# Gated DeltaNet layer: decay masks by GpSimd selection, and the inverse's 64-row block transposed by VectorE

## The chip, the cores and the metric

The kernel runs on one core of a Trainium2 chip. The metric is the device time of one execution in microseconds, the median of three runs. Five engines work side by side: TensorE (PE in the profile, its weight loads PEld), VectorE (DVE), ScalarE (ACT), GpSimd (POOL) and SyncE (SP), which here does nothing but issue DMAs. Each takes its instructions in the order in which they were written and waits on semaphores for the others.

## The reference

One decoder layer over 2048 tokens of width 1024, in float32. The token mixer is a gated DeltaNet of 8 heads of 128, beside it a cross-attention of 4 heads to 256 memory tokens; both read one projection of x, and their outputs are concatenated and projected. Then come a layer norm, an MLP with a squared ReLU (4096 wide) and a second layer norm. The part that matters here is the chunked delta rule, cut to its core:

```
gc = jnp.cumsum(to_chunks(g), axis=-1)
decay = jnp.exp(jnp.where(causal, gc[..., :, None] - gc[..., None, :], -jnp.inf))
lower = jnp.where(strict, jnp.einsum('bnhcd,bnhsd->bnhcs', k_beta, kc) * decay, 0.0)
a_mat = jnp.eye(CHUNK, dtype=f32) + lower
u = lax.linalg.triangular_solve(a_mat, v_beta, ...)
w = lax.linalg.triangular_solve(a_mat, k_beta * jnp.exp(gc)[..., None], ...)
attn_qk = jnp.einsum('bnhcd,bnhsd->bnhcs', qc, kc) * decay
```

and then, chunk by chunk, a state of 128 x 128 per head is read and updated. So each head needs two tables of decays (one strictly lower, one with the diagonal) and, for each chunk, the inverse of a unit lower triangular matrix.

## The kernel before

**Tiling.** Tokens are worked in four blocks of 512 (loop over b at L1111). The kernel uses chunks of 128 tokens in place of the reference's 64, which is the same recurrence, so a block has four chunks per head, side by side in one tile of 128 x 512 (v4, L392). The large matmuls split each float32 operand into a high and a low part of type float32r and add three products (mm3, L468); the high part is a ScalarE cast, the low part a VectorE difference (split, L450), for weights as for activations. The tile of split weights is called whl in the profile, the raw one wraw.

**A block.** For each head, dense (L673) projects q, k, v and z, runs the short convolution (raw, with three tokens of halo copied in by GpSimd) and makes the head's row scales (rk, vbs, bh, nbe) on GpSimd from sums of squares (ss) at L718 to L729. gdn_a (L818) makes the decay tables dl and at, multiplies them with the products of k and q (pkq) and calls invert. gdn_b (L869) runs the four chunks through the state. In step t of the loop at L1127, gdn_b of head t-2, gdn_a of head t-1 and dense of head t are written down one after another; four memory attentions go into the last steps. Then come the output projection (L1141), the layer norm and the MLP (ff_seven, L991).

**The decay tables.** Tile gb holds, in every partition, the cumulated gate of the block's tokens, spread by a DMA (L824). VectorE adds a mask tile m_l (1e30 on and above the diagonal) or m_at (-1e30 below it), repeated for the four chunks, and ScalarE takes the exponential chunk by chunk, with the partition's own gate as the bias.

**invert (L732).** The 128 x 128 triangular matrices of four chunks are inverted together. First all 16-row diagonal blocks, by a substitution of 15 steps on VectorE (shuffle, multiply, subtract on tiles Bc and Xc). Then three rounds of block merging: 16 to 32, 32 to 64, 64 to 128 rows. Each round is two groups of four small float32 matmuls: pq from the off-diagonal block, copied to Q by ScalarE, and pp from the diagonal inverse and Q. The matmul takes its first operand transposed, so each round needs the transposed inverse so far (XB, X32, X64), while Y3 gathers the result. In the last round the 64-row blocks of Y3 are transposed by TensorE into px and copied into X64 by VectorE. pq, px and pp of a head all live in the one PSUM bank of its parity ("ga0" or "ga1"), one after another.

**FF2.** ff_seven multiplies 2 x 2 blocks with seven products instead of eight, accumulating three PSUM results A, B and C (A in the "ga" banks, B and C in the two "pb" banks), which are added to the output tile after every product that contributes. SEVEN (L987) lists the seven in order: left operand, right operand, result, whether it goes on from the last content of the bank, and the output block. Right operands 1 to 4 are sums of weight blocks. In block 0 VectorE makes them (keep_sums, L971) and a DMA writes them to the DRAM scratch tsc, from which they're read there and in the later blocks; B11, B21 and B22 are read as they are.

**What sets the order.** Nothing is issued where it is written. A Recorder (L135) collects all instructions with their data dependences, prices each with a formula of its own (cost, L184), and plays the program as a list schedule (issue, L220): of the instructions that are ready on an engine, the one written first goes next, and tile buffers are handed out in order of first use. The resulting order is then emitted, all of it at L320, which is why most rows of the profile have this line; they're told apart by tile names. The prices decide only the order; on the chip the semaphores decide the times.

## Time and profile before

| | |
|---|---|
| median of three runs | 2998.03 us (2996.6 to 2998.27) |
| the profiled execution | 2999.08 us, its span 2997.4 us |
| granted TensorE clock, mean | 0.995 |
| TensorE busy | 2945.4 us (98%) |
| VectorE busy | 2168.6 us (72%) |
| ScalarE busy | 1520.3 us (51%) |
| GpSimd busy | 332.4 us (11%) |

A row of the profile gives line, engine, operation, output tile and input tiles, shapes, the count, then busy time in us and the mean ns of one, then the idle time of the engine ahead of these instructions and what ended most of it. Matmuls are pipelined: one lasts longer than the distance to the next, so the busy time of a group is less than count times mean. Rows of waits give who waited for whom, the total in us, how often, and the longest. Rows of a timeline give start and duration in us.

### The profile page before, as it was taken

To read this page: it belongs to the slowest core of one execution; us is meant where nothing else is said; L and a number is where in the kernel's file an instruction comes from. 1 tells how busy PE (TensorE), PEld (TensorE's weight loads), DVE (VectorE), ACT (ScalarE), POOL (GpSimd) and SP (SyncE) were. 2 spreads that over 40 slices of the span, in tenths; PEclk is the share of its full clock that TensorE was granted. 3 is DMA by queue.
4 is the path that set the end of the run, shared out by engine and by line. 5 is a ranking of instruction groups with operands and counts; after the bars stand their busy time and mean duration, and the time that the engine had idled before them with its cause. 6 is when DMAs were issued, how large, how long until landed. Compare 5 with 4: busy or idle time off the path is not lost.

```text
span 2997.4 us, 43880 instructions
## 1 busy us (share of the span) xinstructions
PE 2945.4 (98%) x15300; PEld 2428.1 (81%) x15300; DVE 2168.6 (72%) x5537; ACT 1520.3 (51%) x3582; POOL 332.4 (11%) x808
## 2 busy tenths in 40 slices
PE   7999999999999999999999999999999999999998
PEld 6888788888788878888878887888878888788886
DVE  6898977666777787655577887665667787675667
ACT  5676534544355562544445665344554556444443
POOL 1222100000112211000012221000001222000000
PEclk9999999999999999999999999999999999999999
DMA  6765566656733223444473332244446332324443
GB/s 231 253 218 180 196 209 224 200 183 192 268 142 132 106 89 102 145 137 133 151 268 130 121 119 92 87 152 144 145 159 250 126 134 96 99 88 146 143 147 134
DMA packets 127709, 469.85 MB, mean 157 GB/s; under 512 B 14464, under 2 KB 16896, under 8 KB 109056
## 3 DMA queue, kind: packets, MB, share of 16 engines
q1 hardware_dynamic: 126912, 467.00, 46.2%
q8 instruction: 120, 1.97, 0.3%
q14 instruction: 101, 0.83, 0.1%
q10 hardware_dynamic: 576, 0.06, 0.0%
HBM read 402.97 MB, written 64.03 MB: 156 GB/s over the span
## 4 chain that ended last, share of the span: by engine, by line
PE 88%; DVE 8%; ACT 2%; issue 1%; DMA 1%; POOL 0%; POOLq 0%; ACTq 0%; DVEq 0%; SPq 0%
PE af L320 42%; PE ao L320 8%; PE aq L320 6%; PE ak L320 5%; PE az L320 5%; PE av L320 4%; PE amq L320 3%; PE pc L320 3%; PE pp L320 2%; PE pq L320 2%; PE po L320 2%; PE pkq L320 1%; DVE y L320 1%; PE sps L320 1%; DVE ck L320 1%
## 5 line engine op out<-in xcount | busy, mean ns | idle before, releaser
L320 DVE TENSOR_TENSOR whl<-wraw,whl 128x1024 fp32r<-128x1024 f32 (+1 forms) x446 | 538.7, 1216 | 392.8 <-ACT whl L320 386.1
L320 PE MATMUL af<-Thi,whl 128*128 128x512 f32 (+1 forms) x2304 | 655.9, 369 | 6.9 <-DVE whl L320 4.0
L320 ACT CAST whl<-wraw 128x1024 fp32r<-128x1024 f32 (+1 forms) x446 | 466.1, 1045 | 381.8 <-PE af L320 169.0
L320 PEld LDWEIGHTS af<-Thi,whl 128*128 128x128 f32 x2304 | 421.7, 191 | 78.5 <-DVE whl L320 4.8
L320 PE MATMUL af<-whl,xh 128*128 128x512 f32 x1536 | 476.4, 391 | 3.6 <-DVE whl L320 3.6
L320 PE MATMUL af<-Tlo,whl 128*128 128x512 f32 (+1 forms) x1152 | 424.8, 369 | 0.0
L320 PE MATMUL af<-whl,xl 128*128 128x512 f32 x896 | 347.3, 390 | 0.0
L320 PEld LDWEIGHTS af<-whl,xh 128*128 128x128 f32 x1536 | 288.6, 188 | 68.6 <-DVE whl L320 6.7
L320 PE MATMUL ao<-whl,ch 128*128 128x512 f32 x768 | 249.4, 399 | 0.5 <-DVE y L320 0.5
L320 PEld LDWEIGHTS af<-Tlo,whl 128*128 128x128 f32 x1152 | 220.4, 191 | 34.8
L320 ACT ACTIVATE rl<-af 128x512 f32<-128x512 f32 x128 | 76.5, 598 | 271.0 <-PE af L320 269.0
L320 DVE SCALAR_TENSOR_TENSOR y<-y,af 128x512 f32<-128x512 f32 x224 | 151.3, 684 | 84.1 <-PE af L320 82.9
L320 PEld LDWEIGHTS af<-whl,xl 128*128 128x128 f32 x896 | 168.5, 188 | 35.5
L320 POOL TENSOR_SCALAR ve<-mv 128x1 f32<-128x1 f32 x34 | 23.3, 684 | 1528.8 <-DVE mv L320 1528.8
L320 PE MATMUL aq<-Thi,whl 128*128 128x512 f32 x512 | 181.6, 414 | 7.5 <-ACT Thi L320 7.5
L320 PE MATMUL av<-Thi,whl 128*128 128x512 f32 x512 | 173.0, 402 | 0.0
L320 PE MATMUL ak<-Thi,whl 128*128 128x512 f32 x512 | 172.9, 401 | 0.0
L320 PE MATMUL az<-Thi,whl 128*128 128x512 f32 x512 | 170.2, 400 | 0.0
L320 PEld LDWEIGHTS ao<-whl,ch 128*128 128x128 f32 x768 | 142.6, 188 | 27.0 <-DVE y L320 0.7
L320 PE MATMUL ao<-whl,cl 128*128 128x512 f32 x384 | 153.5, 400 | 0.0
L320 PEld LDWEIGHTS aq<-Thi,whl 128*128 128x128 f32 x512 | 94.3, 192 | 21.5 <-ACT Thi L320 7.5
L320 PEld LDWEIGHTS az<-Thi,whl 128*128 128x128 f32 x512 | 95.9, 190 | 18.8 <-DVE whl L320 0.5
(252 smaller groups left out, 5756.3 us busy)
## 6 DMA issues: line engine op xcount, KB each, us to landing
wraw<-in_w_ff_dram SPq DMA_DIRECT2D x224, 512.0 KB, 4.0
whl<-wsc SPq DMA_DIRECT2D x108, 1024.0 KB, 4.8
wraw<-tsc SPq DMA_DIRECT2D x128, 512.0 KB, 3.3
wsc<-whl SPq DMA_DIRECT2D x36, 1024.0 KB, 4.9
wraw<-in_w_out_dram SPq DMA_DIRECT2D x48, 512.0 KB, 4.1
wraw<-in_w_in_dram SPq DMA_DIRECT2D x35, 512.0 KB, 5.8
wq<-in_w_ff_dram SPq DMA_DIRECT2D x64, 256.0 KB, 4.3
tsc<-wq SPq DMA_DIRECT2D x64, 256.0 KB, 3.3
```

Of the source, the lines that this page charges most:

```text
L320: o.fn(*[res(a) for a in o.args], **{k: res(v) for k, v in o.kw.items()})
```

## The change

The tiles m_at and m_l are gone, and so is the addition on VectorE. GpSimd's affine_select copies gb into dl (or at) and fills the masked places with 1e30 (or -1e30) as it goes, by comparing partition and column, over all four chunks in one instruction. The planner gets a price for it.

In invert, X64 is no longer the transposed 64-row block of Y3. Its two diagonal blocks of 32 rows are copied from Z by GpSimd, right behind the same copies into X32. Its off-diagonal block is the transposed pp of the round before: VectorE transposes it in 32 x 32 squares out of PSUM (into t32, which lies in the buffer of Lq, unused by then), and a second VectorE instruction writes it, times -1, into X64. The four TensorE transposes into px and the copy of px are gone.

In FF2, for the first group of the first block alone, the seven products are taken in another order: A12 x B21, the sixth, comes second.

Besides, a padding tile of 112 columns and its memset are gone, and the two buffers of raw become 56 columns longer each, so that the tiles behind them lie at other addresses.

```diff
@@ -215,6 +215,8 @@
             return 300 + 165 * n
         if name == "tensor_copy":
             return 119 + 3.34 * n
+        if name == "affine_select":
+            return 90 + 1.6 * n
         return 150 + 2.1 * n if name == "tensor_tensor" else 176 + 3.34 * n
 
     def issue(self):
@@ -369,8 +371,6 @@
     cst = ctx.enter_context(tc.tile_pool(name="cst", bufs=1))
     wp = ctx.enter_context(tc.tile_pool(name="wp", bufs=1))
     tp = ctx.enter_context(tc.tile_pool(name="tp", bufs=1))
-    pad = ctx.enter_context(tc.tile_pool(name="pad", bufs=1))
-    nc.vector.memset(pad.tile([P, 112], F32, name="shift"), 0.0)
     sp = ctx.enter_context(tc.tile_pool(name="sp", bufs=1))
     sm = ctx.enter_context(tc.tile_pool(name="sm", bufs=1))
     ps = ctx.enter_context(tc.tile_pool(name="ps", bufs=1, space=bass.MemoryType.PSUM))
@@ -400,14 +400,6 @@
     triu = cst.tile([P, P], F32, name="triu")
     nc.gpsimd.affine_select(out=triu, in_=ones, compare_op=ALU.is_ge, fill=0.0,
                             base=0, pattern=[[1, P]], channel_multiplier=-1)
-    m_at = cst.tile([P, P], F32, name="m_at")
-    nc.gpsimd.memset(m_at, 0.0)
-    m_l = cst.tile([P, P], F32, name="m_l")
-    nc.gpsimd.memset(m_l, 0.0)
-    nc.gpsimd.affine_select(out=m_at, in_=m_at, compare_op=ALU.is_ge, fill=-1e30,
-                            base=0, pattern=[[1, P]], channel_multiplier=-1)
-    nc.gpsimd.affine_select(out=m_l, in_=m_l, compare_op=ALU.is_gt, fill=1e30,
-                            base=0, pattern=[[-1, P]], channel_multiplier=1)
     half = cst.tile([P, 2], F32, name="half")
     nc.vector.reduce_sum(out=half, in_=ident.rearrange("p (q h i) -> p h q i", h=2, i=16),
                          axis=AX.XY)
@@ -683,8 +675,8 @@
                 nc.vector.scalar_tensor_tensor(out=c, in0=th, scalar=1.0, in1=a, op0=ALU.add, op1=ALU.mult)
             else:
                 gi = o // P + h
-                raw = rec.buf(tp, (P, TB + 3), F32, "raw", 2, "raw")
-                nc.scalar.copy(out=raw[:, 3:], in_=a)
+                raw = rec.buf(tp, (P, TB + 3 + 56), F32, "raw", 2, "raw")
+                nc.scalar.copy(out=raw[:, 3:TB + 3], in_=a)
                 nc.gpsimd.tensor_copy(raw[:, 0:3], halo[:, gi].part(gi))
                 if b < NB - 1:
                     nc.gpsimd.tensor_copy(halo[:, gi].part(gi), raw[:, TB:TB + 3])
@@ -780,26 +772,27 @@
         nc.vector.transpose(Z.rearrange("p c f -> p (c f)"), ZT.rearrange("p c f -> p (c f)"))
         for p in range(2):
             nc.vector.tensor_copy(X32[32 * p:32 * p + 32, :, 32 * p:32 * p + 32], Z[64 * p:64 * p + 32])
+            nc.gpsimd.tensor_copy(X64[32 * p:32 * p + 32, :, 32 * p:32 * p + 32], Z[32 * p:32 * p + 32])
         for r in quads:
             nc.scalar.copy(out=Y3[r, :, r], in_=ZT[r])
         pq = bank("pq", "ga%d" % par)[:64, :P].rearrange("p (c f) -> p c f", c=NC)
         for c in range(NC):
             nc.tensor.matmul(pq[:, c], L32[:, c], ZT[:, c], start=True, stop=True)
         nc.scalar.copy(out=Q[:64, :, :32], in_=pq)
-        pp = bank("pp", "ga%d" % par)[:64, :P].rearrange("p (c f) -> p c f", c=NC)
+        p32 = bank("pp", "ga%d" % par)
+        pp = p32[:64, :P].rearrange("p (c f) -> p c f", c=NC)
         for c in range(NC):
             nc.tensor.matmul(pp[:, c], X32[:, c], Q[:, c, :32], start=True, stop=True)
+        t32 = Lq[:32].rearrange("p f c -> p (f c)")
+        nc.vector.transpose(t32, p32[:32, :P])
         for p in range(2):
             nc.vector.tensor_scalar_mul(Y3[64 * p:64 * p + 32, :, 64 * p + 32:64 * p + 64],
                                         pp[32 * p:32 * p + 32], -1.0)
+        nc.vector.tensor_scalar_mul(X64[32:64, :, :32], t32.rearrange("p (c f) -> p c f", c=NC), -1.0)
 
         pq = bank("pq", "ga%d" % par)[:64, :2 * P].rearrange("p (c f) -> p c f", c=NC)
         for c in range(NC):
             nc.tensor.matmul(pq[:, c], L[:, c, :64], Y3[:, c, 64:], start=True, stop=True)
-        px = bank("px", "ga%d" % par)[:64, :2 * P].rearrange("p (c f) -> p c f", c=NC)
-        for c in range(NC):
-            nc.tensor.transpose(px[:, c], Y3[:64, c, :64], ident[:64, :64])
-        nc.vector.tensor_copy(X64[:64], px)
         nc.scalar.copy(out=Q[:64], in_=pq)
         pp = bank("pp", "ga%d" % par)[:64, :2 * P].rearrange("p (c f) -> p c f", c=NC)
         for c in range(NC):
@@ -834,12 +827,14 @@
         bh, vbs = r["bh"], r["vbs"]
         dl = slot("dl", "s%d" % par)
         dl3 = v4(dl)
-        nc.vector.tensor_tensor(out=dl3, in0=gb3, in1=m_l.unsqueeze(1).to_broadcast([P, NC, P]), op=ALU.add)
+        nc.gpsimd.affine_select(out=dl3, in_=gb3, compare_op=ALU.is_gt, fill=1e30,
+                                base=0, pattern=[[0, NC], [-1, P]], channel_multiplier=1)
         for c in range(NC):
             nc.scalar.activation(dl3[:, c], dl3[:, c], AF.Exp, bias=sc("gc", c), scale=-1.0)
         at = slot("at", "s%d" % par)
         at3 = v4(at)
-        nc.vector.tensor_tensor(out=at3, in0=gb3, in1=m_at.unsqueeze(1).to_broadcast([P, NC, P]), op=ALU.add)
+        nc.gpsimd.affine_select(out=at3, in_=gb3, compare_op=ALU.is_ge, fill=-1e30,
+                                base=0, pattern=[[0, NC], [1, P]], channel_multiplier=-1)
         for c in range(NC):
             nc.scalar.activation(at3[:, c], at3[:, c], AF.Exp, bias=sc("ngc", c))
         kh, kl = r["kq"]
@@ -973,7 +968,7 @@
         if j == 0:
             B = [t[:, n * TB:(n + 1) * TB].part(n) for t in (tok_tile("wq"), tok_tile("wq")) for n in range(2)]
         else:
-            B = [rec.buf(tp, (P, TB + 3), F32, "raw", 2, "wq")[:, :TB] for _ in range(2)]
+            B = [rec.buf(tp, (P, TB + 3 + 56), F32, "raw", 2, "wq")[:, :TB] for _ in range(2)]
             kq = rec.buf(tp, (P, 2, TB), F32, "kq1", 1, "wq")
             B += [kq[:, n].part(n) for n in range(2)]
         for n in range(4):
@@ -1039,7 +1034,8 @@
             if last:
                 gb = load_bcast(ln2_g, "l2g"), load_bcast(ln2_b, "l2b")
             banks = {}
-            for n, (xn, wn, bn, on, (th, nh)) in enumerate(SEVEN):
+            order = [0, 5, 1, 2, 3, 4, 6] if b == 0 and g == 0 else range(7)
+            for n, (xn, wn, bn, on, (th, nh)) in enumerate(SEVEN[i] for i in order):
                 if not on:
                     banks[bn] = [bank("af2", ("ga%d" % t) if bn == "A" else "pb") for t in range(2)]
                 w = [None, None]
```

## The prediction

> **What bounds the kernel now.** I read the page first, then the list of who waited for whom on TensorE, then the windows.
>
> ```profile
> span 2997.4 us, 43880 instructions
> ...
> PE 2945.4 (98%) x15300; PEld 2428.1 (81%) x15300; DVE 2168.6 (72%) x5537; ACT 1520.3 (51%) x3582; POOL 332.4 (11%) x808
> ...
> PEclk9999999999999999999999999999999999999999
> ...
> PE 88%; DVE 8%; ACT 2%; issue 1%; DMA 1%; POOL 0%; POOLq 0%; ACTq 0%; DVEq 0%; SPq 0%
> ```
>
> TensorE is busy for 2945.4 of 2997.4 us, at nearly full clock throughout; the chain that ended last runs 88% through it. 52 us are left in which it does nothing. So a shorter VectorE, ScalarE or GpSimd instruction is worth only what it takes out of those 52 us, and a TensorE instruction that is dropped is worth its own slot. The waits say how little the first kind can be:
>
> ```profile
> PE af L320 <- DVE whl L320: 7.6, 10, 1.5
> PE aq L320 <- ACT Thi L320: 7.5, 1, 7.5
> ...
> PE pp L320 <- ACT Q L320: 1.6, 6, 0.3
> ...
> PE pkq L320 <- ACT jq L320: 1.2, 1, 1.2
> PE pc L320 <- ACT vt L320: 1.2, 5, 0.4
> ...
> PE pq L320 <- DVE Bc L320: 1.1, 3, 0.4
> ```
>
> (total us, times, longest.) In the chunk stage, the place of the change, the quoted waits of pp, pkq, pc and pq come to 1.6 + 1.2 + 1.2 + 1.1 = 5.1 us in all 32 head-blocks together. The long one, 7.5 us, is the start, where ScalarE's first cast is awaited. In the windows a GDN stretch of the second block looks like this (us; busy us of PE, PEld, DVE, ACT, POOL; clock; DMA share; GB/s):
>
> ```profile
> 800.00:1090.00 290.00, 286.44 (x1679) 234.82 (x1678) 224.99 (x863) 168.25 (x562) 63.48 (x175) 1.00 0.37 133
> ```
>
> TensorE 99% busy, VectorE 225/290 = 78%, GpSimd 22%: the dense projections fill TensorE's time while the heads' chains run.
>
> **Part 1: the 64-row block's transposes leave TensorE.** Per head-block four px transposes, their copy out of PSUM and the bank's hand-over go.
>
> ```profile
> L320 PE MATMUL px<-ident,Y 64*64 64x64 f32 x128 | 14.3, 224 | 0.0
> ```
> ```profile
> 2581.85 0.40 PE L320 MATMUL ao<-whl,cl 128*128 128x512 f32 x1
> 2582.18 0.41 PE L320 MATMUL px<-ident,Y 64*64 64x64 f32 x4
> 2582.52 0.74 PE L320 MATMUL ao<-whl,ch 128*128 128x512 f32 x2
> 2583.10 0.40 PE L320 MATMUL ao<-whl,cl 128*128 128x512 f32 x1
> 2583.34 0.40 PE L320 MATMUL ao<-whl,ch 128*128 128x512 f32 x1
> 2583.66 0.50 PE L320 MATMUL pp<-Q,X 128*64 128x64 f32 x5
> ```
> ```profile
> 508.96 0.39 PE L320 MATMUL af<-whl,xl 128*128 128x512 f32 x1
> 509.19 0.62 PE L320 MATMUL af<-whl,xh 128*128 128x512 f32 x2
> 509.64 0.39 PE L320 MATMUL af<-whl,xl 128*128 128x512 f32 x1
> ```
>
> Undisturbed 512-column matmuls start every (509.64 - 508.96)/3 = 0.227 us. With the four transposes between them two matmuls start 2582.52 - 2581.85 = 0.67 us apart, so the group costs 0.67 - 0.227 = 0.44 us: the run itself is 0.34 (2582.18 to 2582.52), the rest is the change to it. Times 32: **14.2 us**. Lower end 32 x 0.34 = 10.9, if the change of operand is paid by another group then; upper end 14.3, the busy time of the group. I take 14.2, since the group stands alone between dense matmuls. Nothing has to hide this saving: four ao matmuls stand between px and pp, so TensorE wasn't waiting there.
>
> In exchange VectorE transposes the first 32 partitions of pp and scales the result into X64; GpSimd copies two blocks of Z. The nearest rows:
>
> ```profile
> L320 DVE TENSOR_TENSOR at<-gb,m_at 128x512 f32<-128x512 f32 x32 | 22.0, 686 | 3.8 <-PE amv L320 3.6
> ...
> L320 DVE TENSOR_TENSOR dl<-gb,m_l 128x512 f32<-128x512 f32 x32 | 21.8, 684 | 0.0
> ...
> L320 DVE TENSOR_SCALAR Y<-pp 32x128 f32<-32x128 f32 x64 | 18.0, 281 | 9.8 <-PE pp L320 8.7
> ...
> L320 DVE COPY X<-px 64x256 f32<-64x256 f32 x32 | 13.3, 416 | 14.8 <-PE px L320 14.4
> ...
> L320 DVE STREAM_TRANSPOSE Z<-ZT 128x128 f32<-128x128 f32 x32 | 9.8, 306 | 0.2
> ```
>
> VectorE per head: out go 0.416 and, by part 2, 0.686 + 0.684; in come 0.306 (the same 128 elements a partition, though out of PSUM) and 0.281. Net -1.2 us, 38 us over 32 heads, none of it on the bound. The head's chain changes too: pq, Q, px, X64, pp one after another in one bank become pq, Q, pp. It loses 0.34 + 0.416 and gains 0.306, which stands ahead of the two scalings that release pq: 0.45 us shorter. Worth between 0 and the 5.1 us of chunk-stage waits; I take 0, as the chain is mostly covered.
>
> **Part 2: the masks move to GpSimd.**
>
> ```profile
> L320 POOL COPY L<-dl 32x128 f32<-32x128 f32 x64 | 31.2, 487 | 24.7 <-PE pq L320 14.9 <-DVE Bc L320 7.5
> ...
> L320 POOL MEMSET Y<- 128x512 f32 x32 | 16.6, 524 | 49.0 <-DVE R L320 22.2 <-PE amv L320 20.0 <-PE pc L320 6.8
> ...
> L407 POOL TENSOR_SCALAR_AFFINE_SELECT m_at<-m_at 128x128 f32<-128x128 f32 x1 | 0.3, 292 | 0.0
> ```
> ```profile
> L320 POOL COPY LB<-dl x128: 226/235/1359, 78.8 to 2548.0; 32x64 f32<-32x64 f32 x128
> ```
>
> A selection over 512 columns isn't in the trace. It isn't shorter than the write-only 0.524 and not longer than 4 x 0.292 = 1.17, undisturbed; the new price in the diff, 90 + 1.6n ns, gives 0.295 at 128 columns, as the row has, and 0.91 at 512: I take that. The last row shows (min/median/max) that a GpSimd copy of 0.235 can last 1.359, so the upper end of one is 1.17 + 1.12 = 2.3. Per head GpSimd gains 2 x 0.91 + 2 x 0.487 = 2.8 us, 90 us in all: eight heads in the window above take it from 63 to 86 of 290 us, still 30%. What counts is who stands behind the selections in its queue, the row scales of the head:
>
> ```profile
> 2361.43 0.23 POOL L320 TENSOR_SCALAR ss<-ss 128x8 f32<-128x8 f32 x1 [21.38 <-ACT jq L320]
> ...
> 2365.24 0.20 POOL L320 TENSOR_TENSOR nbe<-bh,neg 128x4 f32<-128x4 f32 x1
> ```
> ```profile
> 2362.03 0.68 DVE L320 TENSOR_TENSOR dl<-gb,m_l 128x512 f32<-128x512 f32 x1
> ...
> 2365.20 0.61 DVE L320 SCALAR_TENSOR_TENSOR dl<-pkq,bh,dl 128x128 f32<-128x128 f32 x2
> ```
>
> From 2361.43 to 2365.44 GpSimd makes the scales, bh among them, that the product at 2365.20 reads, and just there the mask was put in. Two selections ahead of them delay this head's product by up to 1.8 us, behind them by as much. VectorE then holds at that product, with the weight splits behind it that TensorE reads. Cover: the dense matmuls whose weights are already split, and the 1.2 us that VectorE gets back. I take 0; without the cover it is rival C.
>
> The two mask tiles, their four GpSimd instructions and the pad's memset at the start cost nothing either way: the 7.5 us wait for ScalarE's cast covers them. The shifted addresses have no row that prices them; I take 0.
>
> **Part 3: the first FF2 group's order.** In block 0, group 0, A12·B21 moves from sixth to second, ahead of the products that need the sums of weights, which are made, written and read back at that time.
>
> ```profile
> 512.97 0.63 PE L320 MATMUL af<-whl,xh 128*128 128x512 f32 x2
> 513.89 0.51 PE L320 MATMUL af<-whl,xh 128*128 128x512 f32 x1 [0.29 <-DVE whl L320]
> ...
> 519.01 0.61 PE L320 MATMUL af<-whl,xh 128*128 128x512 f32 x2
> 521.09 0.50 PE L320 MATMUL af<-whl,xh 128*128 128x512 f32 x1 [1.47 <-DVE whl L320]
> ```
>
> The gaps beyond two slots are 0.47 and 1.63 us: up to 2.1 to gain, as two loads of unsummed weights pass the reads of the sums in SP's queue. Against it: now B hands its banks to C at once and S1 hands A to S4, with no product between.
>
> ```profile
> L320 DVE TENSOR_TENSOR whl<-wraw,whl 128x1024 fp32r<-128x1024 f32 (+1 forms) x446 | 538.7, 1216 | 392.8 <-ACT whl L320 386.1
> ...
> L320 DVE SCALAR_TENSOR_TENSOR y<-y,af 128x512 f32<-128x512 f32 x224 | 151.3, 684 | 84.1 <-PE af L320 82.9
> ```
>
> A bank's add takes 0.684 while TensorE does six matmuls of the other (1.36 us): hidden, unless a split of 1.216 stands ahead: 1.90 - 1.36 = 0.54 us, at most four times, 2.2 us. Between -2.1 and +2.2 I take -1.0, as the largest stop is a load that comes late.
>
> **The sum.** The profiled execution took 2999.08 us (span 2997.4 and 1.7 around it); 2999.08 - 14.2 - 1.0 = 2983.9. The median of the runs, 2998.03, lies 1.05 under that execution: **2983 us**, 0.5% less.
>
> **The rivals.**
>
> A. TensorE's slot isn't freed but idled: with px gone, TensorE waits that long for Q ahead of pp. For it: 1.6 us of waits on Q already. Against it: the four ao matmuls ahead of pp. All 14.2 us back: 2997, no change.
>
> B. The shorter chain also takes out the chunk stage's waits and the whole of part 3: 14.2 + 5.1 + 2.1 = 21.4, so 2977. For it: VectorE's 38 us. Against it: other waits come up when one goes.
>
> C. Slower: the selections come late in GpSimd's queue (the place above) and VectorE's product holds up the splits. If one selection of 0.91 per head reaches TensorE: 32 x 0.91 = 29 us, 2983 + 29 = 3012. It turns the sign from 15/32 = 0.47 us per head on. For it: the copies of up to 1.359 us and the tight place at 2362 us. Against it: TensorE's 99% in the window, with VectorE's own selections just as late today.
>
> The Trainium skill ("SBUF — State Buffer", "Who interferes with whom") speaks for C: a VectorE instruction with two SBUF inputs and a GpSimd one that reads SBUF exclude each other for a whole instruction, whoever starts first. The stretched copies agree with one direction of it; that VectorE stands still behind a long GpSimd read no row here shows. By that rule the 64 selections could cost VectorE up to 64 x 0.91 = 58 us, more than the 38 it gets back.
>
> **How the numbers follow.** Forecast 0.73, A 0.09, B 0.11, C 0.07. Forecast's own ends: -10.9 + 2.2 = -8.7, 2989, and -14.3 - 2.1 = -16.4, 2982 with B's side down to 2977. The range reaches a little beyond both, 2974 to 2993, and leaves out C, most of A, and about 2 in 10 in all. This kernel's measurement tells 0.2%, 6 us, from no change: forecast and B are faster (0.84), A is the same (0.09), C slower (0.07).
>
> **What would show it.** Right: no px rows, TensorE busy about 14 us less with as much idle time as before (52 us), VectorE some 38 us less, 64 selections of about 0.91 us. Part 3: no stop over 1 us in the FF2 group after 490 us. A would show as new waits of pp for Q. C as waits of dl or at for GpSimd, stretched selections, and TensorE's waits for whl above 7.6 us. Wrong altogether if TensorE's idle time grows by as much as its busy time falls.

## The result and the profile after

The changed kernel took 2983.27 us (median; 2980.53 to 2984.46), the kernel before 2998.15 beside it (2996.6 to 2998.39): ratio 0.995, 95% interval 0.9933 to 0.9967. That is 15 us less, as forecast, at 2983.27 against 2983. The experiments show that the terms behind the number were not all right: errors of some 2 to 7 us each cancelled, and that they did is luck.

The page of the kernel after (its profiled execution took 2984.46 us; busy us and share of the span by engine, then the chain that ended last):

```profile
span 2982.7 us, 43804 instructions
...
PE 2927.5 (98%) x15172; PEld 2424.5 (81%) x15172; DVE 2149.5 (72%) x5504; ACT 1520.5 (51%) x3582; POOL 385.3 (13%) x932
...
PE 89%; DVE 7%; ACT 2%; DMA 1%; issue 1%; POOL 0%; SPq 0%; POOLq 0%; ACTq 0%; DVEq 0%
```

TensorE is busy 17.9 us less (2945.4 to 2927.5) and idle 3.2 us more (52.0 to 55.2): the span is 14.7 us shorter. GpSimd is busy 52.9 us more, where I had worked out 90. VectorE's busy time falls by 19.1 us, half of the 38 that I had worked out. Yet the instructions come out as priced, by these groups of after (busy us, mean ns | idle before):

```profile
L322 POOL COPY X<-Z 32x128 f32<-32x128 f32 x64 | 25.0, 390 | 118.3 <-DVE Z L322 112.5 <-DVE Xc L322 3.9
...
L322 DVE STREAM_TRANSPOSE Lq<-pp 32x128 f32<-32x128 f32 x32 | 9.7, 302 | 11.8 <-PE pp L322 11.2
...
L322 DVE TENSOR_SCALAR X<-Lq 32x128 f32<-32x128 f32 x32 | 7.0, 218 | 0.6
```

VectorE loses 22.0 + 21.8 + 13.3 = 57.1 us of instructions and gets 9.7 + 7.0 = 16.7, so 40.4 less. Records of one engine overlap, and the page counts a stretch that two of them cover once. In before's timeline the mask's sum that the prediction quotes at 2362.03 lasts 0.68 us, and the next VectorE instruction starts at 2362.62, before its end. Summed record by record, VectorE falls by 39.3 us. So the forecast was right for the instructions and wrong for the line in which I said it would be seen.

The two selections by tile (min/median/max in ns; first to last start in us):

```profile
L322 POOL TENSOR_SCALAR_AFFINE_SELECT dl<-gb x32: 629/639/1607, 58.3 to 2493.9; 128x512 f32<-128x512 f32 x32
L322 POOL TENSOR_SCALAR_AFFINE_SELECT at<-gb x32: 629/636/1086, 61.4 to 2503.5; 128x512 f32<-128x512 f32 x32
```

0.64 us each undisturbed, where I took 0.91; the longest, 1.607, lies under my contended upper end of 2.3.

Who waited on TensorE in after, and for which GpSimd results VectorE waited (total us, times, longest):

```profile
PE af L322 <- DVE whl L322: 9.5, 9, 2.4
...
PE pq L322 <- DVE Xc L322: 2.6, 4, 1.9
...
PE pp L322 <- ACT Q L322: 1.1, 2, 0.7
```
```profile
DVE dl L322 <- POOL m L322: 5.9, 3, 2.0
...
DVE dl L322 <- POOL bh L322: 3.3, 5, 0.8
```

pp's wait for Q has not grown (1.6 to 1.1 us), so rival A is out. The waits of dl for GpSimd, named as C's sign, are there, small, and for the scales (m, bh), not for the selections. af waits 9.5 us where it waited 7.6, the third of C's signs; without the new FF2 order (e4 below) it is 7.9.

**By block.** The four blocks run the same work on other tokens, except that block 0 also projects the memory's keys and values (amk, amv: 2392 matmuls in its first part against 2236). Blocks 1 to 3 are called the clean blocks below. I cut the trace at each block's first aq matmul and at its last ao matmul (us): the *GDN part* lies between them, the *FFN part* goes from the last ao to the next block's first aq (in block 3 to the last matmul). This is my working from the starts of the matmuls.

| kernel | GDN part, blocks 0 / 1 / 2 / 3 | FFN part, blocks 0 / 1 / 2 / 3 |
|---|---|---|
| before | 437.5 / 399.4 / 399.6 / 399.7 | 338.6 / 334.5 / 334.5 / 333.8 |
| after | 441.5 / 393.9 / 393.8 / 393.8 | 341.2 / 333.7 / 332.2 / 333.0 |

The windows of the GDN parts of blocks 1 and 0, before and then after (from:to; us, busy us of PE, PEld, DVE, ACT, POOL with their instructions; granted clock; DMA share; GB/s):

```profile
783.70:1183.10 399.40, 395.71 (x2236) 323.62 (x2236) 306.02 (x1049) 206.68 (x655) 74.14 (x194) 1.00 0.38 132
7.50:445.00 437.50, 427.10 (x2392) 347.90 (x2393) 371.65 (x1133) 256.24 (x725) 83.10 (x192) 0.99 0.62 216
```
```profile
790.20:1184.10 393.90, 390.65 (x2204) 322.22 (x2203) 301.82 (x1042) 206.38 (x655) 90.06 (x226) 1.00 0.38 134
7.50:449.00 441.50, 428.53 (x2361) 349.98 (x2362) 365.72 (x1123) 257.24 (x725) 99.94 (x224) 0.98 0.61 212
```

Blocks 1 to 3 gained 5.5 to 5.9 us each in the GDN part, and nearly all of block 1's 5.5 is TensorE's busy time (395.71 - 390.65 = 5.1). By the prediction it should have been 8 x 0.44 = 3.5. Block 0 lost 4 us in its GDN part and 2.6 in its FFN part, where it should have gained 3.5 and 1. So two questions were open: why the clean blocks gain more than the slot, and what block 0 loses.

### The profile page after: what moved, and what is told of

It is laid out like the page before. It is cut to its first block, busy times and chain, and to the rows that moved or that the text cites. A ratio compares the mean times of both kernels' runs of the same rounds, so it can differ in the third digit from the quotient of the medians.

```text
span 2982.7 us, 43804 instructions
## 1 busy us (share of the span) xinstructions
PE 2927.5 (98%) x15172; PEld 2424.5 (81%) x15172; DVE 2149.5 (72%) x5504; ACT 1520.5 (51%) x3582; POOL 385.3 (13%) x932
## 4 chain that ended last, share of the span: by engine, by line
PE 89%; DVE 7%; ACT 2%; DMA 1%; issue 1%; POOL 0%; SPq 0%; POOLq 0%; ACTq 0%; DVEq 0%
PE af L322 42%; PE ao L322 9%; PE aq L322 6%; PE az L322 6%; PE ak L322 5%; PE av L322 4%; PE pc L322 3%; PE amq L322 3%; PE pq L322 2%; PE pp L322 2%; PE po L322 2%; PE pkq L322 1%; DVE y L322 1%; DVE whl L322 1%; PE pmo L322 1%; PE sps L322 1%
## 5 line engine op out<-in xcount | busy, mean ns | idle before, releaser
L322 PE MATMUL aq<-Thi,whl 128*128 128x512 f32 x512 | 175.0, 409 | 7.5 <-ACT Thi L322 7.5
L322 PEld LDWEIGHTS av<-Thi,whl 128*128 128x128 f32 x512 | 95.1, 188 | 18.5 <-issue 0.5
```

What stands on the lines that cost most here:

```text
L322: o.fn(*[res(a) for a in o.args], **{k: res(v) for k, v in o.kw.items()})
```

## The experiments

Medians in us; every kernel's ratio is against the kernel before on the same chip, whose median was 2997.68 (e1 to e4), 2998.52 (e5 to e8) and 2998.02 (e9 to e12). An interval of a ratio here is some 3 to 5 us to either side, so medians that lie 2 or 3 us apart are not told apart by their times alone; the block times (from the one profiled execution of each kernel), where three equal blocks agree, tell less than 1 us.

Part of every difference is the granted clock. By the clock records of the traces each execution has stretches of 3.4 to 13.7 us in which half the clock is granted; such a stretch costs up to half its length. Up to the last matmul they add up to 20.5 us in before's profiled execution, 34.1 in after's, 13.7 in e1's, 27.3 in e4's, 10.2 in e5's and e9's, 6.8 in e6's and 17.1 in e7's.

### One part at a time

**e1, the inverse's edit alone**

```diff
+            nc.gpsimd.tensor_copy(X64[32 * p:32 * p + 32, :, 32 * p:32 * p + 32], Z[32 * p:32 * p + 32])
...
+        nc.vector.transpose(t32, p32[:32, :P])
...
+        nc.vector.tensor_scalar_mul(X64[32:64, :, :32], t32.rearrange("p (c f) -> p c f", c=NC), -1.0)
...
-            nc.tensor.transpose(px[:, c], Y3[:64, c, :64], ident[:64, :64])
-        nc.vector.tensor_copy(X64[:64], px)
```

> The kernel before with the inverse's edit alone (X64 by GpSimd copies and a VectorE transpose, no px); masks and FF2 order as before. Slot theory (the forecast): 14.2 us less than before, about 3.6 us in each of the four blocks, idle time of TensorE unchanged. Rival (the head's shorter chain also removes stops): 18 to 21 us less, mostly in blocks 1 to 3, as the trace after the change shows there (6.4, 8.1 and 6.8 us less a block) and block 0 not slower.

Measured 2981.24 (2979.72 to 2984.79), ratio 0.9947 (0.9933 to 0.9962): 16.4 us less. GDN parts 433.1 / 394.9 / 395.0 / 395.0, so 4.4 to 4.7 less in each block. (Block 0's 4.4 has 1.7 us of clock in it: a stretch of low clock at 34 us lasts 6.8 us in before and 3.4 in e1.) The gain lies between the slot's 14.2 and the rival's 18.

**e2, the masks alone**

```diff
-        nc.vector.tensor_tensor(out=dl3, in0=gb3, in1=m_l.unsqueeze(1).to_broadcast([P, NC, P]), op=ALU.add)
+        nc.gpsimd.affine_select(out=dl3, in_=gb3, compare_op=ALU.is_gt, fill=1e30,
+                                base=0, pattern=[[0, NC], [-1, P]], channel_multiplier=1)
```
(and the same for at, and the planner's price)

> The kernel before with GpSimd's selections alone. Slot theory: within 2 us of before. Rival (the 1.4 us a head that VectorE gets back shortens the stops): 5 to 7 us less, in blocks 1 to 3. Rival (the selections hold GpSimd's queue or VectorE up): block 0, where VectorE is fullest, gets 5 to 10 us longer, with new waits of pq for VectorE there.

Measured 2998.18 (2996.34 to 3001.42), ratio 1.0001 (0.9992 to 1.0011): nothing. GDN parts 433.9 / 400.6 / 400.9 / 400.4: block 0 gains 3.6, the others lose 1 each.

**e3, the order in FF2 alone**

```diff
-            for n, (xn, wn, bn, on, (th, nh)) in enumerate(SEVEN):
+            order = [0, 5, 1, 2, 3, 4, 6] if b == 0 and g == 0 else range(7)
+            for n, (xn, wn, bn, on, (th, nh)) in enumerate(SEVEN[i] for i in order):
```

> The kernel before with the new order of the first FF2 group alone. Forecast: 1 us less (between 2.1 less and 2.2 more). Rival (the stops only move to the products that follow): the same as before, within 1.5 us, with stops of 1 to 2.5 us at other products of that group, as in the trace after the change.

Measured 2997.55 (2996.31 to 2999.73), ratio 1.0 (0.999 to 1.001): nothing. Its stops in that group (TensorE's timeline; start, us, what it is, idle before it):

```profile
514.05 0.49 PE L320 MATMUL af<-whl,xh 128*128 128x512 f32 x1 [1.45 <-DVE whl L320]
...
521.30 0.51 PE L320 MATMUL af<-whl,xh 128*128 128x512 f32 x1 [1.45 <-DVE whl L320]
```

Before had one stop of 1.47 and two of 0.29. The order took out none of the first kind and made a second, as the rival in the expectation said.

**e4, the whole change without the order**

```diff
-            order = [0, 5, 1, 2, 3, 4, 6] if b == 0 and g == 0 else range(7)
+            order = range(7)
```

> The changed kernel with the old FF2 order in all groups. Forecast: 1 us slower than the changed kernel, so 2984 to 2985. Rival (the order edit costs, by two stops of 1.5 and 2.4 us and the low clock behind them): 1 to 3 us faster than the changed kernel, 2980 to 2982.

Measured 2979.76 (2979.19 to 2980.73), ratio 0.9941 (0.9926 to 0.9956): 3.5 under after. The stops of that group in after:

```profile
511.49 0.70 PE L322 MATMUL af<-whl,xh 128*128 128x512 f32 x2 [0.31 <-DVE y L322]
...
517.34 0.50 PE L322 MATMUL af<-whl,xh 128*128 128x512 f32 x1 [2.42 <-DVE whl L322]
...
528.89 0.50 PE L322 MATMUL af<-whl,xh 128*128 128x512 f32 x1 [1.46 <-DVE whl L322]
```

and in e4:

```profile
512.34 0.58 PE L322 MATMUL af<-whl,xh 128*128 128x512 f32 x1 [2.28 <-DVE whl L322]
```

4.19 us of stops with the order, 2.28 without it. The edit touches the FFN part of block 0 alone, and that lasts 341.2 us in after and 338.5 in e4, with the same two stretches of low clock of 3.4 us in both: 2.7 us for the order.

Why the order doesn't help is seen in before, on ScalarE and on VectorE ahead of the stop that ends at 521.09 us:

```profile
515.80 1.05 ACT L320 CAST whl<-wraw 128x1024 fp32r<-128x1024 f32 x1 [4.88 <-DMA wraw<-tsc]
```
```profile
517.85 0.69 DVE L320 SCALAR_TENSOR_TENSOR y<-y,af 128x512 f32<-128x512 f32 x1 [1.68 <-PE af L320]
519.21 0.69 DVE L320 SCALAR_TENSOR_TENSOR y<-y,af 128x512 f32<-128x512 f32 x1 [0.67 <-PE af L320]
519.82 2.35 DVE L320 TENSOR_TENSOR whl<-wraw,whl 128x1024 fp32r<-128x1024 f32 x2
```

The weights had landed by 515.80 and their cast was done at 516.85 us (casts and splits paired in order), but the split behind it starts at 519.82, after two adds for which VectorE waited 1.68 and 0.67 us on TensorE. So the stop comes from VectorE's queue, not from a load. In after the split that ends the stop of 2.42 us starts at 516.07, 6 us behind its cast (done at 510.02), after seven sums of weights that fill VectorE from 511.86 on.

**e7, the old addresses**: e4 with the padding tile and the two mask tiles back (they're written, but nothing reads them) and raw 56 columns shorter. TensorE's matmuls come in the same order as in e4.

```diff
+    pad = ctx.enter_context(tc.tile_pool(name="pad", bufs=1))
+    nc.vector.memset(pad.tile([P, 112], F32, name="shift"), 0.0)
...
-                raw = rec.buf(tp, (P, TB + 3 + 56), F32, "raw", 2, "raw")
+                raw = rec.buf(tp, (P, TB + 3), F32, "raw", 2, "raw")
```

> The changed kernel with the old FF2 order (2980 us) and with the old addresses: pad, mask tiles and the length of raw as before the change; every engine's order of work is the same as there. If addresses cost nothing: the same time, block 0 with the same stops at 330 and 369 us. Rival (addresses matter): over 3 us away from it.

Measured 2978.41 (2977.63 to 2980.57), ratio 0.9936 (0.9919 to 0.9952). 1.3 us under e4, inside the intervals; blocks 1 to 3 have the same GDN parts within 0.3 us (393.6 / 394.1 / 393.7). The FFN parts aren't the same. Here is that of block 1 in e4, then in e7 (columns as in the windows above):

```profile
1180.03:1512.23 332.20, 329.87 (x1552) 275.05 (x1551) 210.55 (x301) 161.92 (x226) 5.65 (x7) 1.00 0.47 149
```
```profile
1177.81:1510.81 333.00, 330.72 (x1553) 275.37 (x1552) 210.49 (x302) 161.67 (x226) 5.65 (x7) 1.00 0.47 149
```

The same matmuls in the same order at full clock last 0.8 us longer with the old addresses. It is so in every kernel but before, whose FFN parts all have a stretch of low clock: an FFN part of block 1 or 2 without a stretch of low clock lasts 333.0 to 333.1 us with the old addresses (e1, e2, e3, e5, e6, e7, e9, e10) and 332.2 with the new (after, e4, e8, e11, e12). Over four blocks the new addresses are worth some 3 us. The medians of e4 and e7 don't show it, as e4's profiled execution has 27.3 us of low clock and e7's 17.1. Why the matmuls come faster isn't shown.

### What px cost: its slot, and where it stands

**e5, a dead px behind pq**: e1, and the four transposes again, into the unused half of the bank that pq has just filled; nothing reads them.

```diff
+        pq, px = pq[:, 0].part(0), pq[:, 1].part(1)
         for c in range(NC):
             nc.tensor.matmul(pq[:, c], L[:, c, :64], Y3[:, c, 64:], start=True, stop=True)
+        for c in range(NC):
+            nc.tensor.transpose(px[:, c], Y3[:64, c, :64], ident[:64, :64])
```

> The kernel with the inverse's edit alone (2981 us), and with the four px transposes put back as dead work: their result goes to the unused half of pq's own bank and isn't read, so that nothing waits for them but TensorE's slots. Slot theory (0.44 us each time): 14.2 us more than that kernel, 2995. Rival (the gain was the shorter chain, the slots were idle anyhow): under 4 us more, 2981 to 2985.

Measured 2988.23 (2987.0 to 2990.53), ratio 0.9969 (0.9957 to 0.9981): 7.0 us above e1. GDN parts of blocks 1 to 3: 398.0 to 398.2, so 3.1 more, 0.39 per head. That is near the slot theory's 0.44; the median, between the two expectations, shows less. In the profiled executions block 0's FFN part is 3.6 us shorter than e1's (337.2 against 340.8): e1 has a stop of 2.95 us and 6.8 us of low clock there, e5 a stop of 0.93 and no low clock.

**e6, a dead px in a turn of its own**: as e5, but px takes the bank between pq and pp, as in the kernel before; it is not copied out.

```diff
+        px = bank("px", "ga%d" % par)[:64, :2 * P].rearrange("p (c f) -> p c f", c=NC)
+        for c in range(NC):
+            nc.tensor.transpose(px[:, c], Y3[:64, c, :64], ident[:64, :64])
```

> The same dead transposes, but into a bank of their own turn behind pq and ahead of pp, as before the change: px waits until ScalarE has copied pq, and pp waits for px; still no copy of px. Slot theory: 14.2 us more than the kernel with the inverse's edit alone, 2995, the same as with the dead transposes in pq's bank. Rival (the bank's turn costs beside the slot): 2 to 4 us more than with the dead transposes in pq's bank, 2997 to 2999.

Measured 2994.87 (2993.28 to 2996.69), ratio 0.9989 (0.998 to 0.9998): 6.6 more than e5. GDN parts of blocks 1 to 3: 400.6 to 400.7, another 2.5, 0.31 per head. The median is the slot theory's 2995, but not equal to e5's, as that theory had it.

At first sight that is the price of the bank's turn: px waits until Q is copied. TensorE's timeline shows another price. The same stretch of before as in the profile of the prediction, another head:

```profile
1010.12 0.62 PE L320 MATMUL amq<-Thi,whl 128*128 128x512 f32 x2
1010.67 0.68 PE L320 MATMUL pq<-Y,dl 128*64 128x64 f32 x8
1011.28 0.50 PE L320 MATMUL amq<-Tlo,whl 128*128 128x512 f32 x1
1011.61 0.63 PE L320 MATMUL amq<-Thi,whl 128*128 128x512 f32 x2
1012.17 0.41 PE L320 MATMUL px<-ident,Y 64*64 64x64 f32 x4
1012.51 0.51 PE L320 MATMUL amq<-Tlo,whl 128*128 128x512 f32 x1
1012.85 0.64 PE L320 MATMUL amq<-Thi,whl 128*128 128x512 f32 x2
1013.32 0.40 PE L320 MATMUL amq<-Tlo,whl 128*128 128x512 f32 x1
```

and the group in e5 (px lies in pq's bank there, so its row is called pq<-ident,Y):

```profile
1003.33 0.40 PE L320 MATMUL az<-Tlo,whl 128*128 128x512 f32 x1
1003.66 0.68 PE L320 MATMUL pq<-Y,dl 128*64 128x64 f32 x8
1004.26 0.41 PE L320 MATMUL pq<-ident,Y 64*64 64x64 f32 x4
1004.61 0.73 PE L320 MATMUL az<-Thi,whl 128*128 128x512 f32 x2
1005.17 0.39 PE L320 MATMUL az<-Tlo,whl 128*128 128x512 f32 x1
```

Count from one start to a start where the dense pace of 0.227 us is reached again. In before, 1010.12 to 1011.61 holds three dense matmuls (0.68) and pq: pq costs 0.81. 1011.61 to 1013.32 holds five (1.14) and px: px alone costs 0.57. In e5, 1003.33 to 1005.17 holds three and pq with px behind it, 1.16 together: there px costs 0.35. By this measure a small group of 64 columns that stands alone between dense matmuls pays some 0.2 us that it doesn't pay behind another of its kind. TensorE counts as busy in it, so no wait shows it. By single starts, 23 of the 32 px groups of before stand alone, at 0.54 to 0.55 us each.

It is part of e5's and e6's difference. None of e5's px groups stands alone; 19 of e6's 32 do, four in each clean block, each with a single dense matmul behind it. At 0.57 - 0.35 = 0.22 each they make up some 0.9 of the 2.5 us. The rest isn't split up: the planner's order differs elsewhere too, and TensorE goes from dense to small matmuls 155 times in e5's block 1 and 160 times in e6's. Most of it is busy time again, 394.68 us in e5's block 1 and 396.87 in e6's.

The price alone is also what e1 gained: 8 x 0.55 = 4.4 us in a GDN part, measured 4.4 to 4.7 in each; 32 x 0.55 = 17.6, measured 16.4. For the last 1.0 us by which after's block 1 is under e1's, and for e2's 1 us, I summed every small group of that part at its own cost standing alone. What is left over, waits and a few places, is 4.6 us in before, 4.6 in e1, 3.7 in after, 5.7 in e2 and 5.9 in e6. It moves by about 1 us per block with whichever order the planner writes; the slots themselves are 127.2 us in before and e2, 122.8 in e1 and after. That e6 still lies 3.6 us under before is the clock: its clean GDN parts are longer than before's (400.6 to 400.7 against 399.4 to 399.7), but behind every GDN part before has 3.4 us of low clock and e6 none, so e6's FFN parts are shorter (337.2 / 333.0 / 333.0 / 332.4 against 338.6 / 334.5 / 334.5 / 333.8).

### What the selections cost VectorE

**e8, each selection twice**: e4, the second one in place on its own result, which leaves the values as they are.

```diff
+        nc.gpsimd.affine_select(out=dl3, in_=dl3, compare_op=ALU.is_gt, fill=1e30,
+                                base=0, pattern=[[0, NC], [-1, P]], channel_multiplier=1)
```
(and the same for at)

> The changed kernel with the old FF2 order (2980 us), each selection done twice, the second in place on its own result (the same values): 64 selections more on GpSimd, 41 us of its time by the trace, and each table 0.64 us later. Forecast (GpSimd is covered): within 3 us of 2980. Rival C (GpSimd's queue and the shared reads reach TensorE): 10 to 30 us more, with longer VectorE instructions of two inputs and TensorE's waits for VectorE above 15 us.

Measured 2986.88 (2983.61 to 2990.13), ratio 0.9963 (0.9948 to 0.9978): 7.1 above e4; GDN parts of blocks 1 to 3: 395.9 / 395.8 / 395.4, about 1.8 more. That lies between the forecast's 3 and C's 10.

**e11, two idle selections a head**: e4, and behind the selection of at two more in place on gb that keep every value. The two tables don't wait for them. ScalarE's exponential of gb into qd does, as it reads what they write: VectorE's waits for qd go from 4.6 us in e4 to 14.2.

```diff
+        for _ in range(2):
+            nc.gpsimd.affine_select(out=gb3, in_=gb3, compare_op=ALU.is_ge, fill=0.0,
+                                    base=1000, pattern=[[0, NC], [1, P]], channel_multiplier=-1)
```

> The changed kernel with the old FF2 order (2980 us), and per head two more selections of 128x512 that leave every value as it is (on gb itself, behind both tables, so that dl and at aren't later by their own chain). If the 7 us of the doubled selections were the tables' lateness: within 2 us of 2980. If GpSimd's queue or its reads beside VectorE's: 3 to 8 us more.

Measured 2985.91 (2985.58 to 2987.4), ratio 0.996 (0.9945 to 0.9975): 6.2 above e4; GDN parts of blocks 1 to 3: 396.9 / 396.8 / 396.8, 2.9 more.

**e12, as much GpSimd time in memsets**: e4, and four memsets a head into a tile of their own. (They write to SBUF, that idle tile; they read nothing. The expectation on record says that they do neither.)

```diff
+        for _ in range(4):
+            nc.gpsimd.memset(small("idle", [P, 2 * P], 1), 0.0)
```

> The same with four GpSimd memsets of 128x256 a head in place of those two selections: the same time on GpSimd (1.24 us against 1.28 by the traces) that writes and reads nothing in SBUF. Queue theory: as with the two idle selections. Shared reads: within 2 us of 2980, and VectorE's small two-input instructions (Bc, Xc) not stretched beyond the changed kernel's.

Measured 2979.73 (2977.84 to 2982.37), ratio 0.9939 (0.9926 to 0.9953): e4's time; GDN parts of blocks 1 to 3 as in e4 (393.9 / 394.1 / 393.8). The added groups, in e11 and then in e12:

```profile
L322 POOL TENSOR_SCALAR_AFFINE_SELECT gb<-gb 128x512 f32<-128x512 f32 x64 | 45.3, 710 | 1.0
```
```profile
L322 POOL MEMSET idle<- 128x256 f32 x128 | 40.0, 312 | 6.5
```

So 45 us more of reading selections came with 6 us more of the kernel's time, and 40 us of memsets with none. The small two-input products of the substitution on VectorE show one way in which the reads get there (min/median/max in ns) in before, after and e11:

```profile
L320 DVE TENSOR_TENSOR Xc<-Xc,Bc x480: 114/186/301, 82.4 to 2569.7; 128x28 f32<-128x28 f32 x32, 128x40 f32<-128x40 f32 x32, 128x52 f32<-128x52 f32 x32, 128x16 f32<-128x16 f32 x29
```
```profile
L322 DVE TENSOR_TENSOR Xc<-Xc,Bc x480: 119/191/669, 81.4 to 2559.0; 128x28 f32<-128x28 f32 x32, 128x40 f32<-128x40 f32 x32, 128x4 f32<-128x4 f32 x29, 128x16 f32<-128x16 f32 x29
```
```profile
L322 DVE TENSOR_TENSOR Xc<-Xc,Bc x480: 119/190/714, 80.8 to 2560.1; 128x28 f32<-128x28 f32 x32, 128x40 f32<-128x40 f32 x32, 128x52 f32<-128x52 f32 x32, 128x4 f32<-128x4 f32 x29
```

Before, the longest of 480 lasted 0.301 us, with selections 0.669 and 0.714, the length of one selection. Counting what these and their partners Bc last beyond the median, where it is over 60 ns: 1.3 us in before, 7.2 in e4, 7.0 in e12, 12.8 in e8, 14.5 in e11 (my working from the records). The stretched time goes with the number of reading selections, not with GpSimd's busy time. This is the rule of the Trainium skill ("SBUF — State Buffer", "Who interferes with whom") that the prediction set against the rows: the direction which no row of before showed is here, and its size is small. What the prediction worked out from it at most, 58 us for 64 selections (41 at the measured 0.64 each), stands against 5.6 (e8) and 7.3 us (e11) of stretched products for 64 more.

How much of the 6 to 7 us of the kernel's time these reads cost is not shown, for the order changed with them. e12's matmuls come in e4's order, one by one; e8's and e11's don't: TensorE goes from dense to small matmuls 147 times in block 1 of e4 and e12, 161 times in e8 and 162 in e11. Of the 3.0 us by which e11's block 1 is longer than e4's, 2.1 are TensorE's busy time with the same matmuls (392.82 against 390.71); of e8's 2.0 it is 1.0 (391.74). And with the same 64 selections a clean GDN part got about 1 us longer in e2 against before and about 1 us shorter in e7 against e1, so an order can move it by that much. What a late VectorE can show on TensorE is the rest, about 1 us of idle time per block, and in e11 the waits for qd are in it too.

### Block 0

**e9, block 0 keeps VectorE's sums**: the inverse's edit everywhere, GpSimd's selections only in blocks 1 to 3; the old FF2 order and addresses.

```diff
+        if G["b"] == 0:
+            nc.vector.tensor_tensor(out=dl3, in0=gb3, in1=m_l.unsqueeze(1).to_broadcast([P, NC, P]), op=ALU.add)
+        else:
+            nc.gpsimd.affine_select(out=dl3, in_=gb3, compare_op=ALU.is_gt, fill=1e30,
+                                    base=0, pattern=[[0, NC], [-1, P]], channel_multiplier=1)
```
(and the same for at)

> The inverse's edit in all blocks, GpSimd's selections in blocks 1 to 3 alone, VectorE's masks in block 0, the old FF2 order and the old addresses. If the selections cost block 0 its 4 us (437.3 us to the end of its output projection with them, 433.1 without): 2974 to 2975, with 433 us there and 394 us in the later blocks. Rival (block 0's stops hang on the order that the planner happens to find): 2978 or more, block 0 anywhere from 433 to 440.

Measured 2975.96 (2975.0 to 2981.05), ratio 0.993 (0.9918 to 0.9943), 7.3 under after: the lowest median of all. GDN parts 434.1 / 393.7 / 394.1 / 393.8: block 0 is back near e1's 433.1, the others stay at after's. TensorE's matmuls come in e1's order in block 0 and in e4's in the others. It has the old addresses; the new ones weren't tried with it.

**e10, e9 with the FF2 order**: e3's diff on e9.

> The same with the new order of the first FF2 group. If the order edit costs where VectorE is late (3.5 us between the changed kernel with and without it): 2 to 4 us more than without it, with a stop of over 2 us in that group. Rival (it does nothing, as alone on the kernel before): within 1.5 us.

Measured 2977.96 (2976.58 to 2981.08), ratio 0.9934 (0.9921 to 0.9948): 2.0 above e9; the FFN part of block 0 is 341.1 us against e9's 339.7, 1.4 more, with the same clock in both. Its first stop in that group lasts 1.88 us, e9's first 0.54; both have one of 1.45 to 1.46 later.

What block 0 lost, in after (TensorE's timeline, then two windows with the same columns as above):

```profile
370.90 0.93 PE L322 MATMUL pq<-ZT,LB 128*112 128x16 f32 x8 [1.85 <-DVE Xc L322]
```
```profile
369.00:382.00 13.00, 11.15 (x49) 8.81 (x48) 8.11 (x26) 5.82 (x19) 0.87 (x2) 0.61 0.25 95
```
```profile
330.00:335.00 5.00, 5.00 (x29) 3.92 (x28) 1.58 (x5) 4.85 (x18) 0.34 (x2) 0.66 0.01 2
```

and at the same places in e9:

```profile
367.63 0.93 PE L322 MATMUL pq<-ZT,LB 128*112 128x16 f32 x8 [0.70 <-DVE nmx L322]
```
```profile
330.00:335.00 5.00, 5.00 (x40) 4.14 (x40) 3.66 (x14) 3.49 (x12) 0.75 (x2) 1.00 0.36 105
366.00:379.00 13.00, 12.30 (x83) 9.35 (x83) 10.69 (x31) 7.25 (x21) 0.57 (x2) 1.00 0.37 124
```

The last head's substitution ends late, TensorE stands for 1.85 us, and then the granted clock is 0.61 over 13 us: 0.39 x 13 = 5.1 us. Around 331 us it is 0.66 over 5 us: 1.7 more. With the longer stop (1.85 - 0.70 = 1.15) that makes 8.0 us; the two GDN parts differ by 7.4. So block 0's loss is mostly clock: with half the length of every stretch of low clock taken off, its GDN part is 431.3 us in after and 430.7 in e9. e4, e7 and e12 have the same stop of 1.85 us at this place, each followed by a stretch of low clock (13.7, 6.8 and 10.2 us); e1, e9 and e10 have neither.

The lateness begins with the selection's place in GpSimd's queue. Here is the last head in the timelines of after, GpSimd, ScalarE and VectorE one by one, and then the mask's sum and the same product in e9:

```profile
321.59 0.25 POOL L322 TENSOR_SCALAR ss<-ss 128x8 f32<-128x8 f32 x1 [12.26 <-ACT jq L322]
...
323.68 0.63 POOL L322 TENSOR_SCALAR_AFFINE_SELECT dl<-gb 128x512 f32<-128x512 f32 x1
```
```profile
328.47 0.41 ACT L322 ACTIVATE dl<-dl,gc 128x128 f32<-128x128 f32 x1
...
333.22 0.39 ACT L322 ACTIVATE dl<-dl,gc 128x128 f32<-128x128 f32 x1
```
```profile
336.82 0.35 DVE L322 SCALAR_TENSOR_TENSOR dl<-pkq,bh,dl 128x128 f32<-128x128 f32 x1
```
```profile
316.92 0.68 DVE L322 TENSOR_TENSOR dl<-gb,m_l 128x512 f32<-128x512 f32 x1
...
329.13 0.33 DVE L322 SCALAR_TENSOR_TENSOR dl<-pkq,bh,dl 128x128 f32<-128x128 f32 x1
```

In after the selection of dl starts at 323.68 us, right among the row scales, for which GpSimd had stood 12.26 us waiting for ScalarE's jq; in e9 VectorE makes the same table at 316.92. ScalarE's exponentials of dl start 4.2 us after the selection has ended and run from 328.5 to 333.6, mixed with other work (4.85 of 5 us busy), and the head's first product starts at 336.8. In e9 the exponentials begin at 322.1, before after's selection has even started, and that product starts at 329.1. So both the place behind the scales and ScalarE's order, as the planner wrote them once the masks stood on another queue, made the head late; what each is worth isn't separated. Whether its price for a selection (0.91 us against 0.64 measured) led it there wasn't tried.

## Why the prediction was right, and where it was not

**Part 1, 14.2 us: right mechanism, undersized term.** Measured alone 16.4. The step "a group costs 0.44 us" read the two starts on either side of px and stopped there. The next start of the quoted rows belongs to it: 2581.85 to 2583.10 holds three dense matmuls, 1.25 - 3 x 0.227 = 0.57. So my upper end of 14.3, the busy time of the group, was no upper end. Taking 0 for the head's shorter chain was right: the left-over waits of block 1 are 4.6 us in before and in e1.

**Part 2, 0: right as a sum, wrong as a picture.** Alone it is 0 (e2). Beside the inverse's edit, e7 against e1 gains about 1 us in each of blocks 1 to 3 and loses 4 in block 0, 3.4 of it in a stretch of low clock of 6.8 us. "The dense matmuls cover the selections" held in the clean blocks, 99% TensorE. It failed in block 0 at the last head, where a stop of under 2 us came with 5 us of lost clock. The step "two selections ahead of them delay this head's product by up to 1.8 us, behind them by as much" was too small there: behind the scales the selection itself came 6.8 us later than VectorE's sum in e9, and the product 7.7. C's mechanisms are both there: the place in GpSimd's queue (and then in ScalarE's), and the shared reads, as stretched products on VectorE whose price on TensorE isn't shown. Together they didn't reach the 15 us that would have turned the sign.

**Part 3, -1.0: wrong sign.** 0 alone, and 3.5 and 2.0 us more in the two pairs with the inverse's edit (intervals overlap; in the FFN part of block 0 the traces have 2.7, 1.4 and, for the order alone, 0.3 us more). The failed step is "the largest stop is a load that comes late": the load was there, and the split of its weights stood in VectorE's queue, which the order of the loads doesn't change. The stop did not go; in after one of 2.42 and one of 1.46 us stand in the group. "No stop over 1 us" was refuted by after's two rows. My bound of 2.2 us more is near the larger of these.

**The sum.** The inverse's edit gave 16.4 instead of 14.2; the selections about -1 us per clean block and less than +1 in block 0, apart from the clock, instead of 0; the order +2.7 instead of -1.0; the addresses, taken at 0, about -3; and low clock, which had no term, up to +6.8 (34.1 against 20.5 us of it, at half). These add up to some -12 to -13 us where the spans differ by 14.7; the rest isn't split up. The total fits better than its terms, and that is luck. B (2977) was what a version without the order and without block 0's stop does: e9, at 2975.96, though not by B's mechanism.

## What to carry to other kernels

Where TensorE is the bound, price a small group from the last dense start before it to the point where the dense pace is back, not to the next start; and know that the same group is cheaper right behind another of its kind. Compare stage by stage and block by block before you believe a total: here +4 and -5.5 us stood side by side under a total that fitted. An edit that is free in a steady block can cost in the fullest one, where a short stop may bring a stretch of low clock, so an offload can be put in the other blocks alone (e9). Before you call a change of a few us an effect of an edit, add up the low clock in both executions, and read a stage that had none: that showed the addresses' 3 us, which the medians hid. Work moved to GpSimd that reads SBUF stretches VectorE's two-input instructions (0.1 us per selection here, on VectorE); work that only writes didn't.

## What of the hardware was not expected

- In block 0, stops of 1.85 to 2.42 us of TensorE were followed by 3.4 to 13.7 us at about half the granted clock, in lengths near multiples of 3.4. One of 1.88 us (e10) was not. The length differs between kernels with the same stop (6.8 in e7, 13.7 in e4). A pair of shorter stops, 0.55 and 1.00 us with 0.5 us of work between them, comes behind the GDN parts of blocks 1 to 3; before's profiled execution has 3.4 us of low clock behind all three pairs, e6's behind none. Executions of one kernel that spread by 4 us (after) show granted clocks of 0.993 to 0.995, the longer ones the lower.
- 64-column groups have a fixed cost of about 0.2 us when they stand alone between dense matmuls, counted as busy. Groups of 128 columns show none: pc costs 0.24 and pto 0.45 alone, and 0.68 standing together (medians of their groups, my working from starts).
- The same matmuls in the same order took 332.2 us or 333.0 us per FFN part with two layouts of the tiles in SBUF (e4, e7).
- A selection of 128 x 512 takes 0.64 us, just over twice the 0.292 of one of 128 x 128, and just under a VectorE sum of the same size (0.684).
